# First modulation's shift and scale in column form in one PSUM bank, and the first two feed-forward blocks without their context part and with k outermost

## The chip, the cores and the metric

The kernel runs on one core of one Trainium2 chip. The metric is the device time of one execution in microseconds, taken as the median of several runs. The core has TensorE (PE, with its weight loads PEld), VectorE (DVE), ScalarE (ACT), GpSimd (POOL) and the queue engine SyncE (SP). Each engine works through its own list of instructions in the order in which the program has them, and waits there for what the other engines and the DMA queues owe it.

## The reference, cut to what matters

Two transformer-like blocks follow each other; the change touches only the beginning of the first one.

```python
def modulate(x, shift, scale):
    return x * (1 + scale) + shift

def ada_params(cvec, w, b):
    m = jax.nn.silu(cvec) @ w + b
    return m.reshape(cvec.shape[0], N_ADA, 1, D_MODEL)      # 9 vectors of 1024

def half_ffn(h, shift, scale, gate, g_pre, g_post, w13, w2):
    u = modulate(rmsnorm(h, g_pre), shift, scale)
    return h + 0.5 * gate * rmsnorm(swiglu(u, w13, w2), g_post)
...
        ml = ada_params(c, w_ada[l], b_ada[l])              # for the 512 latent rows x
        mc = ada_params(c_ctx[None], w_ada[l], b_ada[l])    # for the 256 context rows ctx
        h_lat = half_ffn(h_lat, ml[:, 0], ml[:, 1], ml[:, 2], g[0], g[1], w13_a[l], w2_a[l])
        h_ctx = half_ffn(h_ctx, mc[:, 0], mc[:, 1], mc[:, 2], g[0], g[1], w13_a[l], w2_a[l])
```

So before the first big product can run, two slices of `w_ada` (shift, columns 0 to 1023, and scale, columns 1024 to 2047; 1024 rows each, 8 MB together) have to be read and multiplied with two vectors: the SiLU of `c` and of `c_ctx`.

## The kernel before, in words

A matrix product in float32 accuracy is made of three products of float32r halves: each operand is split into a high part (an ACT copy, `wh`, `uh`, `gh`) and a low part (source minus high, usually on DVE, `wl`, `ul`, `gl`). A scheduler writes out the order of each engine's list when the program is built; the order is then fixed.

`setup` makes the columns `sc` (SiLU of `c` and `c_ctx`, 128 x 16). `ffn_a` then runs the startup. Its parts are:

- `ada_start` (lines 192 to 237). It loops over the eight k blocks `kc` of `w_ada`; each brings two tiles of 128 x 1024 from memory, `r1` (scale) and `r0` (shift). The shift is a TensorE product in row form, `adaR`: the two columns of `sc` are the stationary operand and 512 columns of `r0` stream past. The scale is gathered on DVE in `acc1l` and `acc1c`, one multiply-add of 128 x 1024 for each vector and `kc`. After the last `kc`, the rows are copied out (`rows`), turned into columns by eight small transposes (`adaRT`), and the two `acc1` are summed over the partitions: `acc1l` by transposes and a DVE reduction, `acc1c` by eight products with a column of ones (`adaT`). DVE adds the biases and makes the columns `G1l`, `col0l`, `G1c`, `col0c`.
- Interleaved with it, `norm_T` for the four tiles of `x`: a Square with row sum on ACT (`junk`), the inverse root on DVE and POOL (`ntm`, `ntr`), the scaling on DVE (`xn`), eight TensorE transposes (`ntT`), and the copies into `xT`, one half on DVE and one on ACT.
- `ahead` loads and splits the first two weight tiles, their low parts on POOL. The two tiles of `ctx` are normalised on DVE, ACT and POOL right after.
- `modulated` makes `uh` and `ul` from `xT` for one k block after the other: one ACT pass and two DVE passes of 128 x 512.
- `ffn` computes `w13` in blocks `j` of 128 columns, two halves `q` each: `pa` holds 512 latent columns, `pc` 256 context columns. The loops run over `j`, `q`, `kc` and the three partial products. Block 0 first makes its `pa`, then `first()` (transposes and modulation of the context), then its `pc`. From block 1 on, `pa` and `pc` alternate. A `filler` generator puts the work for the other slices of `w_ada` (`acc2l`, `raw_ada`) between the blocks.

From early in block 2 of the feed-forward part on, both kernels have the same instructions in the same order on every engine, to the end of the program.

Of the kernel before, what the change touches and what calls it, by code (L numbers as in the profile page):

```python
# [27 lines left out]
class Net:  # L28
# [32 lines left out]
                self.wpair[i] = self.wsplit(i)  # L61
        return self.wpair.pop(k)

    def ahead(self, n):
        for i in range(n if self.plan else 0):
            tname, off, ap, shp, nm = self.plan[i]
            self.wload(i, bass.AP(tensor=self.tensors[tname], offset=off, ap=ap), shp, nm)
            self.wpair[i] = self.wsplit(i, self.nc.gpsimd)

    def wload(self, k, src, shape, name):  # L70
        raw = self.wr.tile(list(shape), F32, name="raw_" + name, tag="raw")
# [112 lines left out]
        self.nc.sync.dma_start(t, self.scratch[f"row{idx}{w}"])  # L184
        return t

    ONES = "c"
    CE = 0
    MODP = ""
    AH = 2  # L190

    def ada_start(self, pool):
        nc, a = self.nc, self.a
        pb = [self.bank("adaR") for _ in range(2)]
        sc2 = self.sc.rearrange("p (w k) -> p k w", w=2)
        acc = [pool.tile([P, D], F32, name="acc1" + w) for w in "lc"]
        for kc in range(KC):
            r0, r1 = (pool.tile([P, D], F32, name=f"raw_ada{i}", tag="raw", bufs=8) for i in range(2))
            for i, r in ((1, r1), (0, r0)):
                nc.sync.dma_start(r, a["w_ada"][0, kc * P:(kc + 1) * P, i * D:(i + 1) * D])  # L200
            for i in range(2):
                s = self.sc[:, i * 8 + kc:i * 8 + kc + 1]
                if kc == 0:
                    nc.vector.tensor_scalar_mul(acc[i], r1, s)
                else:
                    nc.vector.scalar_tensor_tensor(acc[i], r1, s, acc[i], op0=ALU.mult, op1=ALU.add)
# [10 lines left out]
        ptv = pt[:, 0:16].rearrange("p (k w) -> p w k", w=2)  # L217
        for i, w in enumerate("lc"):
            o, G = (self.const.tile([P, KC], F32, name=n + w) for n in ("col0", "G1"))
            nc.vector.tensor_add(o, ptv[:, i, :], self.bada[:, 0:KC])  # L220
            if w in self.ONES:
                pt = self.bank("adaT")
                for j in range(KC):
                    nc.tensor.matmul(pt[:, j:j + 1], acc[i][:, j * P:(j + 1) * P], self.ones[:, 0:1], start=True, stop=True)
                nc.vector.tensor_add(G, pt[:, 0:KC], self.bada[:, KC:2 * KC])
            else:
                for half in range(2):
                    pt = self.bank("adaT")
                    for j in range(4):
                        kc = half * 4 + j  # L230
                        nc.tensor.transpose(pt[:, j * P:(j + 1) * P], acc[i][:, kc * P:(kc + 1) * P], self.ident)
                    nc.vector.tensor_reduce(G[:, half * 4:half * 4 + 4], pt.rearrange("p (j n) -> p j n", j=4),
                                            axis=AX.X, op=ALU.add)
                nc.vector.tensor_add(G, G, self.bada[:, KC:2 * KC])
# [15 lines left out]
    def norm_T(self, t, x, pool, xT, xn, eng=None):  # L250
        nc = self.nc
        junk = pool.tile([P, D], BF16, name="junk", tag="s")
# [62 lines left out]
    def ffn(self, uh, ul, NT, w13, w2, finish, es, filler=None, rate=0.0, pending=None, lag=1, first=None):  # L315
# [8 lines left out]
        for gi, ng in enumerate(groups):  # L324
# [1 line left out]
            gh, gl = [], []  # L326
            jj = 0
            while jj < ng:
                m = 2 if pending else 1
                cuts = (0, TL // 2, TL) if pending else (0, TL)  # L330
                W, pa, pc = {}, {}, None
                for j in range(j0 + jj, j0 + jj + m):
                    W[j] = [self.weight(w13[:, q * FF + j * P:q * FF + (j + 1) * P].rearrange("(k p) f -> p k f", p=P),
                                        [P, KC, P], "w13") for q in range(2)]
                    pa[j] = [self.bank("pa") for _ in range(2)]
                if ctx:
                    pc = self.bank("pc").rearrange("p (q n) -> p q n", q=2)

                def product(dsts, j, q, kc):
                    h, l = W[j][q]  # L340
# [3 lines left out]
                                             stop=kc == KC - 1 and wi == 2)  # L344

                each = lambda: ((j, q, kc) for j in W for q in range(2) for kc in range(KC))
                for c0, c1 in zip(cuts, cuts[1:]):
                    if c0 > 0:
                        for f in pending:
                            f()  # L350
                        pending = None
                    for j, q, kc in each():
                        product([(pa[j][q][:, c0:c1], slice(c0, c1))] +
                                ([(pc[:, q, :], slice(TL, T))] if ctx and not first else []), j, q, kc)
                if first:
                    first()
                    first = None
                    for j, q, kc in each():
                        product([(pc[:, q, :], slice(TL, T))], j, q, kc)
                for j in W:  # L360
                    s = ev.tile([P, T], F32, name="s", tag="s")
                    g = ev.tile([P, T], F32, name="g", tag="g")
                    h = gp.tile([P, T], F32R, name="gh", tag="gh")
                    l = gp.tile([P, T], F32R, name="gl", tag="gl")
                    nc.scalar.activation(s[:, :TL], pa[j][0], AF.Silu)
                    nc.vector.tensor_mul(g[:, :TL], s[:, :TL], pa[j][1])  # L366
                    if ctx:
                        nc.scalar.activation(s[:, TL:], pc[:, 0], AF.Silu)  # L368
                        nc.vector.tensor_mul(g[:, TL:], s[:, TL:], pc[:, 1])
                    self.split(h, l, g)  # L370
                    gh.append(h)
                    gl.append(l)
# [65 lines left out]
    def ffn_a(self):  # L438
        nc, a, sc = self.nc, self.a, self.scratch
        with ExitStack() as es:  # L440
            self.aux = self.pool(es, "aux", 3)
            xT = self.big_tile([P, KC, TL + TCX], F32, "xT0")
            with ExitStack() as e2:
# [4 lines left out]
                for t in range(4):  # L448
# [4 lines left out]
                    self.norm_T(t, x, sp, xT, sp.tile([P, D], F32, name="xn", tag="xn", bufs=1))()  # L453
                for _ in ada:
                    pass
                self.ahead(self.AH)
                tail = []
                for t in (4, 5):
                    x = sp.tile([P, D], F32, name="xl", tag="xl", bufs=3)
                    nc.sync.dma_start(x, a["ctx"][0, (t - 4) * P:(t - 3) * P, :])  # L460
                    tail.append(self.norm_T(t, x, sp, xT, self.aux.tile([P, D], F32, name="xn", tag="raw"), self.CE and nc.gpsimd))
# [1990 lines left out]
```

## Time and profile before

| | us |
|---|---|
| median of 3 runs (2620.55 to 2624.85) | 2621.93 |
| span of the profiled execution | 2629.1 |
| first product of the feed-forward part starts | 41.07 |
| PE busy over the span | 2464.9 (94%) |

The profile comes from one execution, whose span, from the first to the last instruction, is 2629.1 us; the page gives no other time of that execution. It is 7.2 us above the median of the runs without a profile. Times in the trace count from the start of the span. "PEclk" is the TensorE clock that was granted, as a share of 2.4 GHz: 1.00 is 2.4 GHz, 0.50 is 1.2 GHz.

### The profile page before, as it was taken

Reading aid. Unit: us, or ns where it says so; the run is one execution under the profiler, and the core shown is the slowest. Engines: PE = TensorE matmul, PEld = TensorE weight load, DVE = VectorE, ACT = ScalarE, POOL = GpSimd, SP = SyncE. Lnnn points to the kernel's source line nnn. Section 1 sums busy time; section 2 is a strip of 40 time slices with the busy share of each in tenths; the row PEclk is TensorE's granted clock in tenths of the full one; section 3 lists DMA queues with packets and bytes.
Section 4 is the critical chain, followed back from the end, with each engine's and each line's share of the span. In section 5 each row is a group of like instructions: output and inputs, shape, how many; then the busy total and the mean of one; then the engine's idle time right before and its main releaser. Section 6 shows DMA issues by size and latency. Waiting matters only on the chain. (4 is left out here: it accounts for less than half of the span.)

```text
span 2629.1 us, 32629 instructions
## 1 busy us (share of the span) xinstructions
PE 2464.9 (94%) x12485; PEld 2036.2 (77%) x12485; DVE 1532.1 (58%) x2408; ACT 988.7 (38%) x1785; POOL 495.4 (19%) x487
## 2 busy tenths in 40 slices
PE   7999999998999999999999999998777899996988
PEld 5888888886889889887888887777666687785666
DVE  7554534357557557665433335535696856547899
ACT  4212111125434444434322223435554344322775
POOL 1000000005000000002200002016555434303342
PEclk8999999998999999999999999999888898996999
DMA  7544625344322222154733334448768688664995
GB/s 260 166 152 130 219 64 189 112 153 136 96 75 62 84 73 73 60 171 165 261 92 96 96 96 134 108 93 108 133 121 181 154 149 176 214 220 159 325 332 218
DMA packets 349769, 388.17 MB, mean 148 GB/s; under 512 B 21367, under 2 KB 280924, under 8 KB 349604
## 3 DMA queue, kind: packets, MB, share of 16 engines
q1 hardware_dynamic: 332880, 326.36, 45.5%
q0 software_dynamic: 16544, 59.57, 6.2%
q8 instruction: 100, 1.64, 0.3%
q14 instruction: 65, 0.53, 0.1%
q10 hardware_dynamic: 180, 0.07, 0.0%
HBM read 325.34 MB, written 60.61 MB: 147 GB/s over the span
## 5 line engine op out<-in xcount | busy, mean ns | idle before, releaser
L43 ACT CAST wh<-raw_w 128x1024 fp32r<-128x1024 f32 x132 | 138.2, 1049 | 620.3 <-PE pc L343 233.1
L44 DVE TENSOR_TENSOR wl<-raw_w,wh 128x1024 fp32r<-128x1024 f32 x130 | 159.4, 1229 | 269.8 <-ACT wh L43 267.0
L93 PE MATMUL acc<-wh,gh 128*128 128x512 f32 x440 | 173.9, 395 | 0.0
L94 PE MATMUL acc<-wl,gh 128*128 128x512 f32 x440 | 173.0, 393 | 0.0
L95 PE MATMUL acc<-wh,gl 128*128 128x512 f32 x440 | 172.8, 393 | 0.0
L343 PE MATMUL pa<-u2h,wh 128*128 128x512 f32 (+1 forms) x384 | 145.0, 381 | 5.7 <-ACT u2h L1048 5.7
L343 PE MATMUL pa<-u2h,wl 128*128 128x512 f32 (+1 forms) x384 | 145.8, 380 | 0.0
L343 PE MATMUL pa<-u2l,wh 128*128 128x512 f32 (+1 forms) x384 | 143.9, 375 | 0.0
L343 PE MATMUL pa<-uh,wh 128*128 128x512 f32 x352 | 142.2, 404 | 1.4 <-ACT uh L310 1.4
L343 PE MATMUL pa<-ul,wh 128*128 128x512 f32 x352 | 139.2, 396 | 0.1
L343 PE MATMUL pa<-uh,wl 128*128 128x512 f32 x352 | 138.8, 395 | 0.0
L366 DVE TENSOR_TENSOR g<-s,pa 128x512 f32<-128x512 f32 x44 | 30.2, 686 | 140.6 <-PE pa L343 139.9
L343 PE MATMUL pc<-uh,wh 128*128 128x256 f32 x352 | 98.5, 280 | 0.1
L343 PE MATMUL pc<-ul,wh 128*128 128x256 f32 x352 | 98.4, 280 | 0.0
L1288 DVE SCALAR_TENSOR_TENSOR cv<-padb,cols,cv 128x512 f32<-128x512 f32 x72 | 80.3, 1115 | 31.0 <-ACT cv L1284 30.3
L343 PE MATMUL pc<-uh,wl 128*128 128x256 f32 x352 | 98.3, 280 | 0.0
L93 PEld LDWEIGHTS acc<-wh,gh 128*128 128x128 f32 x440 | 83.2, 189 | 18.3 <-ACT s L368 0.2
L95 PEld LDWEIGHTS acc<-wh,gl 128*128 128x128 f32 x440 | 82.8, 189 | 18.7 <-DVE gl L44 0.5
L94 PEld LDWEIGHTS acc<-wl,gh 128*128 128x128 f32 x440 | 83.1, 189 | 18.3 <-issue 0.2
L2132 DVE TENSOR_TENSOR mwl<-mgu,mwh 128x1024 fp32r<-128x1024 f32 x50 | 80.9, 1627 | 14.6 <-ACT mwh L2131 14.4
L343 PEld LDWEIGHTS pa<-u2h,wh 128*128 128x128 f32 x384 | 73.0, 192 | 19.2 <-ACT u2h L1048 6.2
L343 PEld LDWEIGHTS pa<-u2l,wh 128*128 128x128 f32 x384 | 73.4, 191 | 15.4 <-DVE u2l L1049 0.5
(944 smaller groups left out, 7273.2 us busy)
## 6 DMA issues: line engine op xcount, KB each, us to landing
raw_ada<-in_w_ada SPq DMA_DIRECT2D x72, 512.0 KB, 5.0
raw_w<-in_w_a SPq DMA_DIRECT2D x66, 512.0 KB, 3.9
raw_w<-in_w_b SPq DMA_DIRECT2D x66, 512.0 KB, 3.8
mdn<-in_expert_w_down SPq DMA_DIRECT2D x16, 1024.0 KB, 6.8
mgu<-in_expert_w_gate SPq DMA_DIRECT2D x16, 1024.0 KB, 8.2
mgu<-in_expert_w_up SPq DMA_DIRECT2D x16, 1024.0 KB, 11.9
raw_wg<-in_w_in SPq DMA_DIRECT2D x16, 512.0 KB, 3.8
raw_wo<-in_w_out SPq DMA_DIRECT2D x16, 512.0 KB, 6.7
```

The source lines that it names most:

```text
L43: self.nc.scalar.copy(hi, src)
L44: (eng or self.nc.vector).tensor_sub(lo, src, hi)
L93: self.nc.tensor.matmul(out, ah, bh, start=start, stop=False)
L94: self.nc.tensor.matmul(out, ah, bl, start=False, stop=False)
L95: self.nc.tensor.matmul(out, al, bh, start=False, stop=stop)
L343: nc.tensor.matmul(dst, w[:, kc, :], u[:, kc, c], start=kc == 0 and wi == 0, stop=kc == KC - 1 and wi == 2)
L366: nc.vector.tensor_mul(g[:, :TL], s[:, :TL], pa[j][1])
L1288: nc.vector.scalar_tensor_tensor(t, pad[:, i:i + TL], w[i], t, op0=ALU.mult, op1=ALU.add)
L2132: (nc.gpsimd if i == 2 and e < 13 and n >= 4 or n in self.PRE else nc.vector).tensor_sub(l, x, h)
```

## The change

`ada_start` keeps one PSUM bank, `adaC`, for the whole modulation. The shift tile is now the stationary operand: for each `kc`, eight products load 128 x 128 of `r0` and stream the two columns of `sc` past it, so that the result is in column form. For `kc` 0 to 6 the scale is gathered on DVE as before; after `kc` 6 both `acc1` are added into the same bank by sixteen products with a column of ones; for `kc` 7 the scale tile goes through TensorE like the shift tile. Two additions read the bank out (`mod0l`, `mod0c`).

For the four tiles of `x`, the scaling `xn` and both copies into `xT` move from DVE to ACT (argument `dve=False`). The first weight tile is asked for ahead of the last pair of `w_ada` tiles, the second behind it, and their low parts are made on DVE. The two tiles of `ctx` are loaded early and normalised in `first()`, in place. The first pass of `ffn` now takes blocks 0 and 1 together: their `pa` with `kc` outside `q`, then `first()`, then their `pc`.

```diff
     def ahead(self, i0, i1):
...
-            self.wpair[i] = self.wsplit(i, self.nc.gpsimd)
+            self.wpair[i] = self.wsplit(i)
...
+    DVE_KC = 7
...
+        def by_pe(r, i, kc):
+            for b in range(KC):
+                nc.tensor.matmul(cols(i, b), r[:, b * P:(b + 1) * P], sc2[:, kc, :], start=i == kc == b == 0, stop=False,
+                                 skip_group_check=True)
+
         for kc in range(KC):
...
-            for hf in range(2):
-                nc.tensor.matmul(pb[hf][0:2, :], sc2[:, kc, :], r0[:, hf * 512:hf * 512 + 512],
-                                 start=kc == 0, stop=kc == KC - 1)
+            rs = [pool.tile([P, D], F32, name=f"raw_ada{i}", tag="raw", bufs=8) for i in range(2)]
+            for i in ((1, 0) if kc < self.DVE_KC else (0, 1)):
+                nc.sync.dma_start(rs[i], a["w_ada"][0, kc * P:(kc + 1) * P, i * D:(i + 1) * D])
+            by_pe(rs[0], 0, kc)
+            if kc >= self.DVE_KC:
+                by_pe(rs[1], 1, kc)
+            else:
+                for i in range(2):
...
+                    if kc == self.DVE_KC - 1:
+                        for b in range(KC):
+                            nc.tensor.matmul(cols(1, b)[:, i:i + 1], acc[i][:, b * P:(b + 1) * P], self.ones[:, 0:1],
+                                             start=False, stop=False, skip_group_check=True)
             yield
-        rows = pool.tile([2, D], F32, name="rows")
-        nc.vector.tensor_copy(rows[:, 0:512], pb[0][0:2, :])
-        nc.scalar.copy(rows[:, 512:], pb[1][0:2, :])
-        pt = self.bank("adaRT")
-        for kc in range(KC):
-            nc.tensor.transpose(pt[:, kc * 2:kc * 2 + 2], rows[:, kc * P:(kc + 1) * P], self.ident[:2, :2])
...
+            og = self.const.tile([P, 2, KC], F32, name="mod0" + w)
+            nc.vector.tensor_tensor(og, pv[:, i], self.bada[:, 0:2 * KC].rearrange("p (i k) -> p i k", i=2), op=ALU.add)
+            o, G = og[:, 0, :], og[:, 1, :]
             nc.vector.scalar_tensor_tensor(G, G, 1.0, self.ng[:, 0:KC], op0=ALU.add, op1=ALU.mult)
...
-        (eng or nc.vector).tensor_scalar_mul(xn, x, r)
+        if dve:
+            nc.vector.tensor_scalar_mul(xn, x, r)
+        else:
+            nc.scalar.mul(xn, x, r)
...
-                if half == 0:
+                if half == 0 and dve:
                     nc.vector.tensor_copy(dst, src)
                 else:
                     nc.scalar.copy(dst, src)
...
-                m = 2 if pending else 1
+                m = 2 if pending or first else 1
...
+                first_order = lambda: ((j, q, kc) for j in W for kc in range(KC) for q in range(2))
...
-                    for j, q, kc in each():
+                    for j, q, kc in each() if not first else first_order():
...
+                for j in W:
+                    s = ev.tile([P, T], F32, name="s", tag="s")
+                    g = ev.tile([P, T], F32, name="g", tag="g")
+                    out[j] = s, g
+                    act(j, s, g, slice(0, TL), pa[j])
                 if first:
                     first()
                     first = None
...
+                for _ in range(4):
+                    next(ada)
+                self.ahead(0, 1)
+                next(ada)
+                self.ahead(1, 2)
+                xc = [self.aux.tile([P, D], F32, name="xc", tag="raw") for _ in range(2)]
...
             def first():
-                for f in tail:
-                    f()
+                junk = self.aux.tile([P, D], F32, name="junkc", tag="raw")
+                for t in range(2):
+                    self.norm_T(t + 4, xc[t], None, xT, xc[t], junk=junk)()
                 self.modulated(xT, uh, ul, *self.LC[1])
```

The list of PE in the startup, before: row-form products (`adaR`), transposes of `x` (`ntT`), and the turn into columns at its end, up to the first products of the feed-forward part (`pa`).

```order
L208 MATMUL adaR<-raw_ada_194,sc 2x512
L263 MATMUL ntT<-ident,xn 128x128 x8
L208 MATMUL adaR<-raw_ada_225,sc 2x512 x2
L208 MATMUL adaR<-raw_ada_233,sc 2x512 x2
L208 MATMUL adaR<-raw_ada_241,sc 2x512 x2
L208 MATMUL adaR<-raw_ada_249,sc 2x512 x2
L208 MATMUL adaR<-raw_ada_257,sc 2x512 x2
L216 MATMUL adaRT<-ident,rows 128x2 x4
L231 MATMUL adaT<-ident,acc1l 128x128 x8
L224 MATMUL adaT<-ones,acc1c 128x1 x8
L216 MATMUL adaRT<-ident,rows 128x2 x4
L343 MATMUL pa<-uh,wh 128x512 x2
```

The same list now, from the products of `kc` 1 on (`raw_ada_168` is `kc` 1's shift tile, `_320` and `_321` are `kc` 7's shift and scale tiles).

```order
L200 MATMUL adaC<-sc,raw_ada_168 128x2 x8
L259 MATMUL ntT<-ident,xn 128x128 x16
L200 MATMUL adaC<-sc,raw_ada_205 128x2 x8
L259 MATMUL ntT<-ident,xn 128x128 x8
L200 MATMUL adaC<-sc,raw_ada_242 128x2 x8
L200 MATMUL adaC<-sc,raw_ada_256 128x2 x8
L200 MATMUL adaC<-sc,raw_ada_270 128x2 x8
L200 MATMUL adaC<-sc,raw_ada_284 128x2 x8
L219 MATMUL adaC<-ones,acc1l 128x1 x8
L219 MATMUL adaC<-ones,acc1c 128x1 x8
L200 MATMUL adaC<-sc,raw_ada_320 128x2 x8
L200 MATMUL adaC<-sc,raw_ada_321 128x2 x8
```

Where two products of 512 columns stood for each `kc`, there are eight of 2 columns, each with a stationary tile of its own, and the sixteen products with `ones` stand ahead of the last two groups instead of behind them.

The list of ACT in the startup, before: Squares (`junk`), copies of transposed tiles (`xT`), the first weight casts and the first modulation (`uh`).

```order
L254 ACTIVATE junk,ss<-xl 128x1024
L269 COPY xT_98<-ntT 128x4x128
L254 ACTIVATE junk,ss<-xl 128x1024
L269 COPY xT_98<-ntT 128x4x128
L254 ACTIVATE junk,ss<-xl 128x1024
L269 COPY xT_98<-ntT 128x4x128 x2
L43 CAST wh<-raw_w_308 128x1024
```

The same stretch now, with the scaling of `x` (`xn`) on this engine; the SiLU that makes `sc` stands two rows ahead of the first of these.

```order
L247 ACTIVATE junk,ss<-xl 128x1024
L265 COPY xT_98<-ntT 128x4x128
L252 ACTIVATE xn<-xl,ntr 128x1024
L265 COPY xT_98<-ntT 128x4x128 x3
L247 ACTIVATE junk,ss<-xl 128x1024
L252 ACTIVATE xn<-xl,ntr 128x1024
L265 COPY xT_98<-ntT 128x4x128 x2
L247 ACTIVATE junk,ss<-xl 128x1024
L252 ACTIVATE xn<-xl,ntr 128x1024
L265 COPY xT_98<-ntT 128x4x128 x2
L43 CAST wh<-raw_w_314 128x1024
```

The Square of the third tile of `x` now stands behind the copies of the second tile's transposes, and the Square of the fourth behind those of the third.

The list of DVE where the context part begins, now: the end of block 0's `pa` (`g`), the normalisation of `ctx` (`ntm`, `xc`), filler work (`acc2l`, `acc2c`), the copies of the context's transposes (`xT`) and its modulation.

```order
L356 TENSOR_TENSOR g<-s,pa 128x512
L104 TENSOR_SCALAR ntm<-ss 128x1 x2
L250 TENSOR_SCALAR xc<-xc,ntr 128x1024 x2
L158 TENSOR_SCALAR acc2l<-raw_ada_701,sc 128x1024
L158 TENSOR_SCALAR acc2c<-raw_ada_701,sc 128x1024
L160 SCALAR_TENSOR_TENSOR acc2l<-raw_ada_705,sc,acc2l 128x1024
L160 SCALAR_TENSOR_TENSOR acc2c<-raw_ada_705,sc,acc2c 128x1024
L356 TENSOR_TENSOR g<-s,pa 128x512
L263 COPY xT_98<-ntT 128x4x128 x2
L160 SCALAR_TENSOR_TENSOR acc2l<-raw_ada_709,sc,acc2l 128x1024
L308 TENSOR_SCALAR xT_98<-xT_98,mod0c_353 128x256 x2
L309 TENSOR_TENSOR ul<-xT_98,uh 128x256 x2
```

Before, the first filler work (`acc2l`) stood behind the whole modulation of the context; now five of its passes stand ahead of it.

## Rows read from the trace of the kernel before

**Rows 1.** The page: busy us and share of the span by engine, with the count of instructions.
```profile
PE   2464.9 (94%) x12485; PEld 2036.2 (77%) x12485; DVE 1532.1 (58%) x2408; ACT 988.7 (38%) x1785; POOL 495.4 (19%) x487
```

**Rows 2.** Timeline, first 25 us: start, duration, engine, line, tiles, count, idle before.
```profile
5.56 0.18 ACT L254 ACTIVATION_READ_ACCUMULATOR junk<-xl 128x1 f32 x1
...
5.78 0.15 DVE L104 TENSOR_SCALAR ntm<-ss 128x1 f32<-128x1 f32 x1 [5.78 <-ACT junk L254]
6.08 0.56 POOL L105 TENSOR_TENSOR ntr<-ntm,mhalf 128x1 f32<-128x1 f32 x1 [4.58 <-DVE ntm L104]
...
7.49 1.69 PEld L263 LDWEIGHTS ntT<-ident,xn 128*128 128x128 f32 x8
...
9.51 3.50 PE L208 MATMUL adaR<-raw_ada,sc 128*2 128x512 f32 x4
...
14.71 1.52 POOL L105 TENSOR_TENSOR ntr<-ntm,mhalf 128x1 f32<-128x1 f32 x1 [2.72 <-DVE ntm L104]
...
17.08 1.09 PE L263 MATMUL ntT<-ident,xn 128*128 128x128 f32 x8 [0.38 <-DVE xn L256]
...
21.37 7.20 PE L208 MATMUL adaR<-raw_ada,sc 128*2 128x512 f32 x16
```

**Rows 3.** Timeline, 29 to 41 us: from the last tile of w_ada to the first product.
```profile
29.29 0.09 PEld L208 LDWEIGHTS adaR<-raw_ada,sc 128*2 128x2 f32 x2 [1.66 <-DMA raw_ada<-in_w_ada]
...
31.57 1.28 DVE L206 SCALAR_TENSOR_TENSOR acc1c<-raw_ada,sc,acc1c 128x1024 f32<-128x1024 f32 x1
...
35.76 3.41 PE L224 MATMUL adaT<-ones,acc1c 128*128 128x1 f32 x16
...
39.10 0.59 PE L216 MATMUL adaRT<-ident,rows 2*128 2x2 f32 x4
...
41.07 1.22 PE L343 MATMUL pa<-uh,wh 128*128 128x512 f32 x2 [1.38 <-ACT uh L310]
```

**Rows 4.** Windows: PE, PEld, DVE, ACT, POOL busy, granted clock, DMA share, GB/s.
```profile
34.00:46.00 12.00, 10.54 (x42) 9.03 (x42) 5.33 (x15) 5.80 (x10) 4.46 (x4) 0.50 0.63 190
752.00:753.00 1.00, 1.00 (x10) 1.00 (x10) 0.16 (x1) 0.52 (x3) 0.33 (x1) 1.00 0.21 55
754.00:756.00 2.00, 2.00 (x11) 2.00 (x11) 0.00 (x0) 1.14 (x4) 0.00 (x0) 0.50 0.90 265
2324.00:2326.00 2.00, 1.96 (x16) 1.86 (x16) 0.61 (x1) 0.77 (x3) 0.00 (x0) 1.00 0.79 220
```

**Rows 5.** Timeline, 752 to 761 us, PE alone.
```profile
752.40 0.27 PE L93 MATMUL S<-qh,kh 128*128 128x128 f32 x1
752.51 0.28 PE L94 MATMUL S<-ql,kh 128*128 128x128 f32 x1
...
756.10 0.41 PE L94 MATMUL S<-ql,kh 128*128 128x128 f32 x1
756.31 0.41 PE L95 MATMUL S<-qh,kl 128*128 128x128 f32 x1
756.53 0.73 PE L561 MATMUL wg<-u1h,wh 128*128 128x512 f32 x1
...
760.41 0.40 PE L561 MATMUL wg<-u1h,wh 128*128 128x512 f32 x1
```

**Rows 6.** Timeline, 2324 us: products of 20 columns.
```profile
2324.02 1.96 PE L1816 MATMUL rbias<-wrt,gbc 128*128 128x20 f32 x16 [0.70 <-DVE gbc L1813]
```

**Rows 7.** Groups of instructions, startup: count, then busy us and mean ns of one.
```profile
L254 ACT ACTIVATE junk<-xl 128x1024 bf16<-128x1024 f32 x4 | 4.2, 1058 | 5.6 <-DMA xl<-in_x 5.6
L269 ACT COPY xT<-ntT 128x512 f32<-128x512 f32 x4 | 2.3, 580 | 3.5 <-PE ntT L263 3.5
```

**Rows 8.** Timeline of ACT: SiLU on the context part of blocks 1, 2 and 3.
```profile
80.95 0.37 ACT L368 ACTIVATE s<-pc 128x256 f32<-128x256 f32 x1
97.75 0.38 ACT L368 ACTIVATE s<-pc 128x256 f32<-128x256 f32 x1
114.55 0.38 ACT L368 ACTIVATE s<-pc 128x256 f32<-128x256 f32 x1
```

More of the change, by code (lines that the diff above doesn't have):

```diff
@@ L62, in weight, with ahead @@
         return self.wpair.pop(k)
-    def ahead(self, n):
-        for i in range(n if self.plan else 0):
+    def ahead(self, i0, i1):
+        for i in range(i0, i1 if self.plan else i0):
             tname, off, ap, shp, nm = self.plan[i]
             self.wload(i, bass.AP(tensor=self.tensors[tname], offset=off, ap=ap), shp, nm)
-            self.wpair[i] = self.wsplit(i, self.nc.gpsimd)
+            self.wpair[i] = self.wsplit(i)
     def wload(self, k, src, shape, name):
@@ L185, in row @@
         return t
-    ONES = "c"
-    CE = 0
     MODP = ""
     AH = 2
+    DVE_KC = 7
     def ada_start(self, pool):
         nc, a = self.nc, self.a
-        pb = [self.bank("adaR") for _ in range(2)]
+        pb = self.bank("adaC")
+        cols = lambda i, b: pb[:, (i * KC + b) * 2:(i * KC + b) * 2 + 2]
         sc2 = self.sc.rearrange("p (w k) -> p k w", w=2)
         acc = [pool.tile([P, D], F32, name="acc1" + w) for w in "lc"]
+        def by_pe(r, i, kc):
+            for b in range(KC):
+                nc.tensor.matmul(cols(i, b), r[:, b * P:(b + 1) * P], sc2[:, kc, :], start=i == kc == b == 0, stop=False,
+                                 skip_group_check=True)
@@ L197, in ada_start @@
         for kc in range(KC):
[L198 to L206, printed above, removed]
@@ L217, in ada_start @@
-        ptv = pt[:, 0:16].rearrange("p (k w) -> p w k", w=2)
-        for i, w in enumerate("lc"):
[L219 to L234, printed above, removed]
+            rs = [pool.tile([P, D], F32, name=f"raw_ada{i}", tag="raw", bufs=8) for i in range(2)]
@@ L248, in slab8, with norm_T @@
         return self.mr.tile(shape, dtype, name=name, tag="dn", bufs=3)
-    def norm_T(self, t, x, pool, xT, xn, eng=None):
+    def norm_T(self, t, x, pool, xT, xn, dve=True, junk=None):
         nc = self.nc
-        junk = pool.tile([P, D], BF16, name="junk", tag="s")
+        if junk is None:
+            junk = pool.tile([P, D], BF16, name="junk", tag="s")
         ss = self.sm.tile([P, 1], F32, name="ss", tag="ss")
@@ L328, in ffn @@
             while jj < ng:
-                m = 2 if pending else 1
+                m = 2 if pending or first else 1
                 cuts = (0, TL // 2, TL) if pending else (0, TL)
-                W, pa, pc = {}, {}, None
+                W, pa, pc = {}, {}, {}
                 for j in range(j0 + jj, j0 + jj + m):
                     W[j] = [self.weight(w13[:, q * FF + j * P:q * FF + (j + 1) * P].rearrange("(k p) f -> p k f", p=P),
-                                        [P, KC, P], "w13") for q in range(2)]
+                                        [P, KC, P], "w13", 1 if first else None) for q in range(2)]
                     pa[j] = [self.bank("pa") for _ in range(2)]
-                if ctx:
-                    pc = self.bank("pc").rearrange("p (q n) -> p q n", q=2)
+                    if ctx:
+                        pc[j] = self.bank("pc").rearrange("p (q n) -> p q n", q=2)
                 def product(dsts, j, q, kc):
@@ L351, in ffn, with act @@
                         pending = None
-                    for j, q, kc in each():
+                    for j, q, kc in each() if not first else first_order():
                         product([(pa[j][q][:, c0:c1], slice(c0, c1))] +
-                                ([(pc[:, q, :], slice(TL, T))] if ctx and not first else []), j, q, kc)
+                                ([(pc[j][:, q, :], slice(TL, T))] if ctx and not first else []), j, q, kc)
+                out = {}
+                def act(j, s, g, c, x):
+                    nc.scalar.activation(s[:, c], x[0], AF.Silu)
+                    nc.vector.tensor_mul(g[:, c], s[:, c], x[1])
+                for j in W:
[3 more added lines that the diff above has]
+                    act(j, s, g, slice(0, TL), pa[j])
                 if first:
@@ L452, in ffn_a @@
                     nc.sync.dma_start(x, a["x"][0, t * P:(t + 1) * P, :])
-                    self.norm_T(t, x, sp, xT, sp.tile([P, D], F32, name="xn", tag="xn", bufs=1))()
+                    self.norm_T(t, x, sp, xT, sp.tile([P, D], F32, name="xn", tag="xn", bufs=2), False)()
+                for _ in range(4):
[5 more added lines that the diff above has]
+                for t in range(2):
+                    nc.sync.dma_start(xc[t], a["ctx"][0, t * P:(t + 1) * P, :])
                 for _ in ada:
                     pass
[L456 to L461, printed above, removed]
                 uh, ul = (self.big_tile([P, KC, TL + TCX], F32R, n) for n in ("uh", "ul"))
@@ L465, in first @@
             def first():
-                for f in tail:
-                    f()
+                junk = self.aux.tile([P, D], F32, name="junkc", tag="raw")
+                for t in range(2):
+                    self.norm_T(t + 4, xc[t], None, xT, xc[t], junk=junk)()
                 self.modulated(xT, uh, ul, *self.LC[1])
```

16 lines of the change are left out of this document (9 added, 7 removed).

## The prediction

> **What bounds the kernel now.** I read the page first. PE is busy for 94% of the span [rows 1], and the change touches only the startup and the first two blocks of the feed-forward part; behind them both programs have the same lists. So the question is one number: how much later or earlier PE reaches block 2. A shift there goes through to the end, since nothing in this program waits for a fixed time.
>
> Then I read the timeline of the startup. Before, its end is a chain. The last tile of `w_ada` is there at 29.29, DVE's last multiply-add ends at 31.57 + 1.28 = 32.85, and then come the copies, transposes and sums, up to the last `adaRT` transposes at 39.10 + 0.59 = 39.69; the first product of the feed-forward part starts at 41.07, 1.38 later [rows 3]. Between the last tile and the last transposes lie 10.4 us, and of these the reader may expect the column form to save most: with the result already in columns, little is left to do behind the last load.
>
> The last thing that I read is the clock, and it decides the case. The first four `adaR` rows take 3.50 us, 0.88 each, and sixteen later ones 7.20, or 0.45 each [rows 2]: by their durations the first run at 1.2 GHz and the later ones at 2.4. From 34 to 46 us, where PE does transposes, the products with `ones` and the first products of block 0, and is busy for most of the time, the granted clock is 0.50 throughout [rows 4].
>
> **The price of a column-form product.** The nearest rows are the eight products with `ones` for `acc1c`: a 128 x 128 float32 tile as stationary operand and one column past it. They are 16 rows (two for each float32 product) and take 3.41 us, 0.213 for a row, at the granted clock of 0.50 [rows 3, 4]. At 1.00 the sixteen `rbias` rows with 20 columns take 1.96, 0.1225 for a row [rows 4, 6]. The weight load sets this pace, not the columns. So eight such products cost 3.41 us at half clock and 1.96 at the full one.
>
> The new startup has 9 groups of eight with `raw_ada` (eight for the shift, one for `kc` 7's scale) and 2 with `ones`: 88 products, 176 rows. At half clock they cost 11 x 3.41 = 37.5 us, at the full one 21.6. The 32 transposes come on top: 1.69 of loads for eight at half clock, 1.09 for eight at the full one [rows 2].
>
> **Which clock they get.** Before, the products that went ahead of the first full-clock rows were the 512-column `adaR`, and these are gone; what is left is transposes and products of one or two columns. The trace has a plain case of this at 752 us. Products of 128 columns follow each other without any gap, PE busy 1.00 and loads 1.00 of each microsecond, and in the middle of it the clock falls from 1.00 to 0.50: a product every 0.11 us at 752.4 and every 0.21 at 756.1 [rows 4, 5]. It is back only after some 3.9 us of 512-column products (756.53 to 760.41) [rows 5]. Together with 34 to 40 us, where products of this very kind ran at 0.50 to the end, it makes me take half clock for the whole startup.
>
> The Trainium skill speaks against this. TensorE: Matmul & The Clock Gate, Part 1 (The HAM clock gate), says that sustained activity releases the throttle and that the instructions are not counted, so an uninterrupted stream of small products would warm the clock as well as any. By that rule PE, busy without a break, would be at 2.4 GHz for most of the startup; the result is the first rival below. The trace does not agree: the unbroken stretch at 752 us lost the full clock. The same page, LDWEIGHTS (loading the stationary operand), gives a load of 128 columns as 128/1.2 = 107 ns; by it the 176 rows would cost an estimated 18.8 us. The rows at half clock have twice that, and the rows decide.
>
> **The startup step by step, at half clock.** The first transposes wait for `xn` from ACT: `ntr` ends at 6.08 + 0.56, an ACT pass of 128 x 1024 takes 1.06 [rows 2, 7], so PE starts at 7.85, has eight transposes until 9.55, `kc` 0 until 12.96, `kc` 1 until 16.37, and the transposes of the second tile until 18.07, the last of them ending some 0.2 later. Now the order bites. The third tile's transposes are next on PE, and ACT's Square of that tile stands behind the copies of the second tile's transposes. PE waits for: a copy 0.58, the Square 1.06 and its sum 0.19, `ntm` 0.15, `ntr` 0.56 to 1.52, the scaling 1.06 [rows 2, 7], and about 0.5, an estimate, for five hand-overs: 4.1 to 5.1, taken as 4.6. It resumes at 22.9 and has the transposes until 24.6 (ending 24.8) and `kc` 2 until 28.0; the fourth tile's chain of 4.6 ends at 29.4. Transposes until 31.1, four groups for `kc` 3 to 6 until 44.7, the two groups with `ones` until 51.6, `kc` 7 twice until 58.4.
>
> The loads don't hold this up: the last tile was there at 29.29 before [rows 3]; now it comes later, since its buffer is released by `kc` 3's products at about 34.5, and a `w_ada` tile landing even 6 us after that is there long before 51.6. What is taken off DVE (four `xn`, four copies, two multiply-adds, the two reductions) is worth nothing here, since PE ends last; the same holds for the low parts that move from POOL to DVE, made under PE's 30 us of products.
>
> From the last product to the first of the feed-forward part I keep the 1.38 of before: 59.8 in place of 41.07, **+18.7 us**. Bounds: without either wait of PE for ACT, 6.2 less (+12.5); with the longer chain twice, about 1 more; at the full clock's price of a row, the first rival below.
>
> **Blocks 0 and 1.** A block takes 114.55 - 97.75 = 16.8 at full clock [rows 8], and the context's sixteen transposes 2.2: 35.8 for two blocks. Before, from 41.07 to the SiLU at 80.95 [rows 3, 8] are 39.9, so 4.1 are lost; most of that is the half clock, which lasts to 46 us at least [rows 4], and waits for `uh` and `ul`. Now the same price of the clock comes again: 3.9 us of dense products in one case [rows 5], at least 4.9 in the other (41.07 to 46), so about 4.4 at half speed, 2.2 lost. With `kc` outside `q` each k block feeds six products, so PE waits less for the modulation; I put the first products' waits at 1.0 (0 to 2, an estimate). Before the context's products PE waits for the copies, ACT and DVE, and DVE's list has a filler pass there whose load goes through one buffer three times in a row: 2.5 (1 to 4, an estimate). With 0.4 until the SiLU the loss is 6.1, against 4.1: **+2.0**. So the k-outermost order gives back what it can, and the new wait for the context takes it again.
>
> **The sum.** 18.7 + 2.0 = +20.7 us. The profiled span is 2629.1, 7.2 above the median; with the change it should read about 2650. On the median that is 2621.9 + 20.7 = **2642.6**, its own range 2635 to 2649.
>
> **The rivals.**
>
> *The full clock in the startup.* `kc` 0 at half clock until 12.96, from there 1.96 for a group and 1.0 for eight transposes: `kc` 1 until 14.9, transposes until 15.9, ACT's chain until 20.6, transposes 21.6, `kc` 2 23.6, chain until 26.3, transposes 27.3, four groups 35.1, two with `ones` 39.1, two for `kc` 7 43.0. That is +3.3 against 39.69, and -0.2 in the blocks, which start warm: 2625. For it: that PE would have no idle stretch from 27 us on. Against it: the two stretches above [rows 4, 5]. It is not slower by what can be told: 0.2%, or 5.2 us, is about what a measurement of this kernel tells from no change. It decides where a group of eight costs about 2.0 in place of 3.4. It is also what the rule of the Trainium skill above would give in this kernel.
>
> *The full clock, and ACT's chain hidden too.* The two waits (4.7 and 2.7) go: the last product at 35.6, -4.1, and -0.2 in the blocks: 2617.6. Even so it is faster by less than 0.2%; for more, PE's rows would have to be cheaper than any row of the trace. I see no such row.
>
> *The clock rises on the way*, say at 31 us, when the long unbroken run begins: the last 27.3 us shrink by 0.1225/0.213 to 15.7, and the blocks start warm: 20.7 - 11.6 - 2.2 = +6.9, 2629. Against it: from 34 to 40 us, 6 us of the same kind did not raise it [rows 4].
>
> *The wait for the context grows*: 3 us more if the filler's load lands late, 2646; inside the range.
>
> **How the numbers follow.** Main case 0.80; full clock 0.09; clock rising on the way 0.07; faster by over 0.2% by something that I don't see 0.04. Slower by over 0.2% is the first and the third, 0.87; the same 0.09; faster 0.04. The range is 2629 to 2649: it holds the main case with its bounds and the lower edge of the third case, and leaves out the other two.
>
> **What would show it.** Right: in the changed profile the `adaC` rows come every 0.21 us to the end, at a granted clock of 0.50 where the trace records one; PE has gaps of 4 to 5 us near 18 us and of 1 to 2 near 28; the last `adaC` row ends at 57 to 60 and the first `pa` row starts about 1.4 later; the SiLU on the context of block 2 starts near 118 instead of 97.75, and everything behind it has the same distance. Wrong: `adaC` rows every 0.12 us, a last one near 43, or a first `pa` row before 45.

## The result, and the profile after

The changed kernel takes 2641.51 us, the median of 10 runs (2634.97 to 2650.04), against 2623.40 for 10 runs of the kernel before beside it (2610.41 to 2633.52). The ratio is 1.0077, its 95% interval 1.0059 to 1.0095, that is 15.5 to 24.9 us slower, 20.2 by the ratio itself; the two medians differ by 18.1. The prediction was 2642.6 with a range of 2629 to 2649.

The page's line of busy time, as in [rows 1] for before:

```profile
PE 2474.1 (94%) x12597; PEld 2060.7 (78%) x12597; DVE 1526.9 (58%) x2395; ACT 994.3 (38%) x1792; POOL 491.9 (19%) x485
```

PE is busy for 9.2 us more, PEld for 24.5: the new products are weight loads above all.

The timeline of PE from the first transposes to the first product of the feed-forward part (start, duration, engine, line, operation, tiles, count, idle before); it answers to [rows 2, 3]:

```profile
7.76 1.97 PE L259 MATMUL ntT<-ident,xn 128*128 128x128 f32 x8
9.52 6.83 PE L200 MATMUL adaC<-sc,raw_ada 128*128 128x2 f32 x32
16.20 1.95 PE L259 MATMUL ntT<-ident,xn 128*128 128x128 f32 x8
22.86 1.97 PE L259 MATMUL ntT<-ident,xn 128*128 128x128 f32 x8 [4.71 <-ACT xn L252]
24.62 3.41 PE L200 MATMUL adaC<-sc,raw_ada 128*128 128x2 f32 x16
29.53 1.97 PE L259 MATMUL ntT<-ident,xn 128*128 128x128 f32 x8 [1.50 <-ACT xn L252]
31.30 13.65 PE L200 MATMUL adaC<-sc,raw_ada 128*128 128x2 f32 x64
44.81 3.55 PE L219 MATMUL adaC<-ones,acc1l 128*128 128x1 f32 x16
48.22 3.55 PE L219 MATMUL adaC<-ones,acc1c 128*128 128x1 f32 x16
51.64 6.96 PE L200 MATMUL adaC<-sc,raw_ada 128*128 128x2 f32 x32
59.98 0.79 PE L339 MATMUL pa<-uh,wh 128*128 128x512 f32 x1 [1.38 <-ACT uh L306]
```

A group of 16 rows costs 3.41 us wherever it stands, also in the stretch from 31.30 to 58.60, in which PE has no gap at all. PE is the engine that ends last: in DVE's timeline the first sum behind the products waits for them, for 21.24 us.

```profile
58.64 0.17 DVE L225 TENSOR_TENSOR mod0l<-adaC,cols 128x16 f32<-128x16 f32 x1 [21.24 <-PE adaC L200]
```

Then PE in block 0, where the full clock comes back (a product every 0.43 us up to 65, every 0.23 from there), and the turn to the context, with a wait of 1.17 behind the sixteen transposes:

```profile
64.44 0.63 PE L339 MATMUL pa<-ul,wh 128*128 128x512 f32 x1
64.86 0.53 PE L339 MATMUL pa<-uh,wl 128*128 128x512 f32 x1
65.24 0.39 PE L339 MATMUL pa<-ul,wh 128*128 128x512 f32 x1
65.47 0.39 PE L339 MATMUL pa<-uh,wl 128*128 128x512 f32 x1
...
85.30 1.91 PE L259 MATMUL ntT<-ident,xc 128*128 128x128 f32 x16
88.38 0.50 PE L339 MATMUL pc<-uh,wh 128*128 128x256 f32 x2 [1.17 <-ACT uh L306]
```

ACT's timeline, the SiLU on the context of blocks 0, 1 and 2 (before: [rows 8], block 2 at 97.75):

```profile
99.31 0.37 ACT L355 ACTIVATE s<-pc 128x256 f32<-128x256 f32 x1
...
103.47 0.37 ACT L355 ACTIVATE s<-pc 128x256 f32<-128x256 f32 x1
...
118.00 0.38 ACT L355 ACTIVATE s<-pc 128x256 f32<-128x256 f32 x1
```

So the first product is 18.9 us later and block 2 20.25 us. The profiled spans differ by less, 2638.3 against 2629.1: 11 us of the shift are not there at the end of this execution. The last experiments are about them.

### The profile page after: what moved, and what is told of

Its sections match the earlier page's. It is cut to its first block, busy times and chain, and to the rows that moved or that the text cites. A ratio compares the mean times of both kernels' runs of the same rounds, so it can differ in the third digit from the quotient of the medians.

```text
span 2638.3 us, 32844 instructions
## 1 busy us (share of the span) xinstructions
PE 2474.1 (94%) x12597; PEld 2060.7 (78%) x12597; DVE 1526.9 (58%) x2395; ACT 994.3 (38%) x1792; POOL 491.9 (19%) x485
## 5 line engine op out<-in xcount | busy, mean ns | idle before, releaser
L93 PE MATMUL acc<-wh,gh 128*128 128x512 f32 x440 | 173.6, 395 | 0.0
L95 PEld LDWEIGHTS acc<-wh,gl 128*128 128x128 f32 x440 | 82.6, 188 | 18.8 <-DVE gl L44 0.5
L2139 DVE TENSOR_TENSOR mwl<-mgu,mwh 128x1024 fp32r<-128x1024 f32 x50 | 80.9, 1627 | 14.7 <-ACT mwh L2138 14.5
L339 PEld LDWEIGHTS pa<-u2h,wh 128*128 128x128 f32 x384 | 72.4, 190 | 19.2 <-ACT u2h L1055 6.1
```

The lines of the kernel that those rows point to most:

```text
L93: self.nc.tensor.matmul(out, ah, bh, start=start, stop=False)
L95: self.nc.tensor.matmul(out, al, bh, start=False, stop=stop)
L339: nc.tensor.matmul(dst, w[:, kc, :], u[:, kc, c], start=kc == 0 and wi == 0, stop=kc == KC - 1 and wi == 2)
L2139: (nc.gpsimd if i == 2 and e < 13 and n >= 4 or n in self.PRE else nc.vector).tensor_sub(l, x, h)
```

## Experiments

The table holds what each run's profile and its times show. "Rest" is the span less the time of block 2's SiLU, and "at 0.50" the part of the rest in which the granted clock is 0.50, added up over the clock events of the trace. Times against before are the ratio and its 95% interval, turned into us by the median of the runs of before beside it. before2, again and warm2 are further profiles of the kernel before, the changed kernel and warm.

| kernel | first product | SiLU, block 2 | rest | at 0.50 | time against before, us |
|---|---|---|---|---|---|
| before | 41.07 | 97.75 | 2531.4 | 196.3 | |
| before2 | 39.20 | 95.11 | 2527.3 | 183.7 | |
| rowform | 39.42 | 99.47 | 2529.2 | 186.6 | +4.7 (1.6 to 7.6) |
| changed | 59.98 | 118.00 | 2520.3 | 177.0 | +20.2 (15.5 to 24.9) |
| again (the changed kernel) | 60.01 | 117.40 | 2504.0 | 150.4 | +19.2 (12.3 to 26.0) |
| colonly | 56.04 | 118.31 | 2521.2 | 186.1 | +17.6 (14.2 to 21.0) |
| prewarm | 57.97 | 116.61 | 2515.3 | 172.7 | +14.2 (10.5 to 18.1) |
| warm | 60.46 | 120.33 | 2496.5 | 136.1 | +7.1 (1.8 to 12.3) |
| warm2 (the same) | 60.41 | 119.86 | 2510.6 | 173.6 | |
| dve8 | 56.44 | 114.94 | 2512.5 | 168.0 | +10.5 (6.3 to 14.4) |
| normdve | 54.23 | 111.42 | 2524.2 | 184.4 | +6.6 (2.9 to 10.0) |
| both | 50.96 | 109.97 | 2522.6 | 184.4 | +3.4 (0.0 to 6.8) |
| qouter | 59.85 | 117.27 | 2517.4 | 174.3 | +16.5 (11.5 to 21.3) |
| delay | 59.81 | 116.57 | 2524.5 | 197.6 | +12.6 (7.9 to 17.3) |

**Which part of the change: rowform and colonly.**

```diff
 # rowform: the changed kernel
-    ada_start with by_pe (column form)
+    ada_start of the kernel before (adaR, adaRT, adaT)
-    xn ... bufs=2
+    xn ... bufs=1     (room for the tile rows)
 # colonly: the kernel before
-    ada_start with adaR, adaRT, adaT
+    ada_start with by_pe, DVE_KC = 7
```

> The startup's modulation is computed in row form again, as before the change; the norms' scaling on ACT, the k-outermost order and the two blocks without ctx stay. My theory (PE's 88 column-form products at 0.21 us a row make the loss): the first product of the feed-forward part starts at 40 to 42 us in place of 59.98, the SiLU on the context of block 2 at 97 to 101, and the time is -2 to +3 us against the kernel before. Rival, the norm's chain on ACT makes the loss: the first product stays behind 47, time +6 or more. Rival, the new order of the first two blocks makes it: the first product at 41, but block 2 more than 5 us late.

> The kernel before with the column form alone. My theory: adaC rows 0.21 us apart, first product of the feed-forward part at 57 to 62 us, time +16 to +21 against the kernel before. Rival, the move of the norms to ACT makes part of the loss: first product before 55, time under +13.

PE in rowform; all of the last 20 adaR rows are one run, and the eight products with `ones` (16 rows) that took 3.41 us in [rows 3] take 1.95:

```profile
24.72 8.75 PE L208 MATMUL adaR<-raw_ada,sc 128*2 128x512 f32 x20
...
36.29 1.95 PE L224 MATMUL adaT<-ones,acc1c 128*128 128x1 f32 x16
39.42 1.22 PE L347 MATMUL pa<-uh,wh 128*128 128x512 f32 x2 [1.18 <-ACT uh L314]
```

Without the column form the 18.9 us are gone, so neither the norms on ACT nor the new loads make them. Block 2 came where my theory had it and the first product 0.6 us before its range; the time is above what it allowed (+4.7 in place of at most +3). Against the second profile of before, block 2 is 4.4 us late, which is nearer to that time. In colonly the products end at 53.1, earlier than in the changed kernel, since PE hardly waits for the norms there; then PE waits 2.95 us for a weight's high part, and the two blocks take longer (62.3 us from the first product to block 2's SiLU; 58.0 in the changed kernel):

```profile
27.44 1.97 PE L257 MATMUL ntT<-ident,xn 128*128 128x128 f32 x8 [1.11 <-DVE xn L250]
...
46.12 6.97 PE L202 MATMUL adaC<-sc,raw_ada 128*128 128x2 f32 x32
56.04 0.79 PE L337 MATMUL pa<-uh,wh 128*128 128x512 f32 x1 [2.95 <-ACT wh L43]
```

The first product lies 1 us below my expectation; block 2 (+20.6) and the time are the changed kernel's within the intervals. The column form alone makes nearly all of the loss; the rest of the change costs 1.7 us at block 2 of rowform by the first profile of before, 4.4 by the second.

**Whether it is the clock: prewarm and warm.** Both add products of 512 bf16 columns whose results nobody uses.

```diff
 # prewarm: the changed kernel
+        self.warm(10)
         nc.tensor.transpose(pt[:, 0:16], cc, ...)
+        self.warm(4)
         nc.tensor.transpose(pt[:, 16:136], v1, ...)
+        self.warm(4)
 # warm: the changed kernel, in by_pe, and the same in the loop with ones
                 nc.tensor.matmul(cols(i, b), r[:, b * P:(b + 1) * P], sc2[:, kc, :], ...)
+                if b % 2:
+                    self.warm(1)
```

> The changed kernel with 18 products of 512 bf16 columns (results unused) ahead of the first transposes, where PE is idle, so that the startup's own products begin at the full clock. My theory: the column-form products do not keep it; the first groups have rows 0.12 us apart, the later ones 0.21; first product of the feed-forward part at 55 to 60, time 0 to -5 against the changed kernel (+13 to +18 against before). Rival, the clock stays once it is up: all rows at 0.12, first product at 43 to 48, time within 5 us of before.

> The changed kernel with one product of 512 bf16 columns (result unused) behind every second column-form product, 44 in all. My theory, the clock sets the row price: from the second or third group on the rows are 0.12 us apart (a group of eight with its four extra products 2.8 us in place of 3.41), first product of the feed-forward part at 50 to 54, and with blocks that begin at the full clock the time is +7 to +12 against before. Rival, the weight load has this price whatever the clock: rows stay at 0.21, first product at 60 or later, time +18 or more.

In prewarm the startup begins at the full clock: eight transposes take 1.04 us in place of 1.97. Within the first column-form group it is lost, and it doesn't come back before the feed-forward part. The timeline of PE:

```profile
8.45 1.04 PE L270 MATMUL ntT<-ident,xn 128*128 128x128 f32 x8
11.26 3.08 PE L211 MATMUL adaC<-sc,raw_ada 128*128 128x2 f32 x16 [1.77 <-ACT sc L147]
...
15.94 3.41 PE L211 MATMUL adaC<-sc,raw_ada 128*128 128x2 f32 x16
```

And two windows of prewarm (PE, PEld, DVE, ACT, POOL busy, granted clock, DMA share, GB/s):

```profile
12.00:52.00 40.00, 37.00 (x175) 36.83 (x175) 16.66 (x17) 10.15 (x16) 3.08 (x2) 0.50 0.71 245
30.00:56.00 26.00, 26.00 (x123) 26.00 (x124) 5.40 (x5) 1.17 (x2) 0.00 (x0) 0.50 0.53 164
```

In 40 us with the loads busy for 36.83 the granted clock is 0.50 throughout, also in the second window, in which PE has no gap. First product (57.97) and time (+14.2) lie where my theory had them; the clock did not even last for the first groups, as it allowed. The Trainium skill, TensorE: Matmul & The Clock Gate, Part 1 (The HAM clock gate), lets sustained activity release the throttle and does not count the instructions; for these products the trace doesn't agree.

In warm my theory expected more than came: the first product is at 60.46, not at 50 to 54. The scheduler did not leave the extra products where I put them; up to 33 us they stand singly and the rows stay slow, then ten and thirteen stand together. PE's timeline:

```profile
32.80 4.28 PE L194 MATMUL dm<-wm 128*128 128x512 bf16 x10
36.91 1.84 PE L208 MATMUL adaC<-sc,raw_ada 128*128 128x2 f32 x16
38.62 2.97 PE L194 MATMUL dm<-wm 128*128 128x512 bf16 x13
...
46.12 2.73 PE L229 MATMUL adaC<-ones,acc1l 128*128 128x1 f32 x16
48.70 3.55 PE L229 MATMUL adaC<-ones,acc1c 128*128 128x1 f32 x16
```

Windows of warm, one in each state:

```profile
36.00:46.00 10.00, 10.00 (x69) 7.47 (x68) 0.00 (x0) 0.00 (x0) 0.00 (x0) 1.00 0.45 154
48.00:58.00 10.00, 10.00 (x48) 10.00 (x48) 0.00 (x0) 0.00 (x0) 0.00 (x0) 0.50 0.17 42
```

Between the extra products the same 16 rows cost 1.84 us. The clock column reads 1.00 there, but the trace has no clock event before the fall near 47 us; it is the rows' durations that show the full clock. At 46.12 the extra products stop, the clock falls within the next sixteen rows, and a group costs 3.55. So the price is the clock's, which the rival (a load of this price at any clock) denied. At 7.1 the time lay at the lower edge of the range that I gave, but not for my reason: the startup gained nothing, the rest of this execution is the shortest of all (2496.5). As a repair the extra products came too late and stopped too early.

**The rows and the waits by themselves: dve8, normdve, both.**

```diff
 # dve8
-    DVE_KC = 7
+    DVE_KC = 8
 # normdve
-    self.norm_T(t, x, sp, xT, sp.tile(..., bufs=2), False)()
+    self.norm_T(t, x, sp, xT, sp.tile(..., bufs=2))()
 # both: the two together
```

> The changed kernel with the scale of the last k block on DVE as well: eight column-form products, 16 rows, fewer. My theory (PE ends last, 0.213 us a row): the last adaC row ends 3.4 us earlier, near 55.2, the first product of the feed-forward part at 56.6, time -3 to -4 against the changed kernel (+14 to +17 against before). Rival, DVE's chain or the loads end last: the first product stays at 59 to 60.

> The changed kernel with the scaling of xn and the first copy of each tile on DVE again, as before the change. My theory: PE's two waits for ACT (4.7 and 1.5 us) all but go, since DVE has room; last adaC row near 53, first product at 54 to 55, time -4 to -6 against the changed kernel (+11 to +15 against before). Rival, the norms end as late on DVE, behind its multiply-adds: the first product stays at 58 to 60.

> The changed kernel with both edits: the last scale block on DVE, and the norms' scaling on DVE. My theory: the two add up, first product at 50.5 to 52, time -8 to -10 against the changed kernel (+8 to +12 against before): the column form still loses, since 160 rows at 0.213 are 34 us. Rival, DVE becomes the bound: first product at 54 or later.

PE in normdve; of the two waits for `xn` one of 1.11 is left, and the last products begin 5.7 us earlier:

```profile
27.26 1.97 PE L259 MATMUL ntT<-ident,xn 128*128 128x128 f32 x8 [1.11 <-DVE xn L250]
...
45.95 6.97 PE L200 MATMUL adaC<-sc,raw_ada 128*128 128x2 f32 x32
```

The first product is 3.5 us earlier in dve8 (16 rows at 0.213 are 3.4), 5.75 in normdve, and 9.0 in both, where the two add up within 0.3: PE ends last, and each row and wait taken from it counts. The times gained more than that: by the table 10, 14 and 17 us against the changed kernel, where 3 to 4, 4 to 6 and 8 to 10 were expected. With some 6 us either way on such a difference dve8 is compatible, normdve and both are not; what their times gained beyond the startup isn't shown. Even so none of them is faster than the kernel before, nor is rowform; no version of the runs beats it.

**The k-outermost order: qouter.**

```diff
-first_order = lambda: ((j, q, kc) for j in W for kc in range(KC) for q in range(2))
+first_order = lambda: ((j, q, kc) for j in W for q in range(2) for kc in range(KC))
```

> The changed kernel with q outside k in the first two blocks, so that a k block of uh and ul feeds three products in place of six. My theory: PE starts at 60 as in the changed kernel and waits some 1 to 2 us more for uh and ul; block 2's SiLU on the context 0 to 2 us later than 118.0; time within 3 us of the changed kernel. Rival, the k-outermost order is worth more than the prediction gave it: 4 us or more later.

From the first product to block 2's SiLU are 57.4 us; in the two profiles of the changed kernel 58.0 and 57.4. Block 2 is 0.7 us earlier than in the first of these, where my theory had 0 to 2 later and the rival 4 or more. The order of q and k makes no difference that can be seen: PE waits 0.52 us for `ul` in either.

**Whether a shift goes through: delay, again, before2, warm2.**

```diff
 # delay: the kernel before
-                for j in range(KC):
+                for j in list(range(KC)) * 7:
                     nc.tensor.matmul(pt[:, j:j + 1], acc[i][:, j * P:(j + 1) * P], self.ones[:, 0:1], ...)
```

> The kernel before with one thing added: the eight products with ones for acc1c are issued seven times over (the same result each time), 96 more rows at some 0.213 us, so that all behind the startup comes about 20 us later and nothing else is changed. If a shift of the startup goes through to the end, as the prediction says: block 2's SiLU on the context near 118, time +19 to +22. Rival, part of any such shift is given back later, where TensorE's clock falls at other places: the same SiLU near 118, time +10 to +16, and fewer us at the granted clock of 0.50 behind block 2 than in the kernel before.

> The changed kernel once more, beside the delayed one. By the prediction's step: +18 to +21 against before. If the falls of the clock behind block 2 go by where the work stands, its profile has them at the same places as the first one (877, 979 and 1085 us, none near 773); if they are chance, at others.

> The kernel before once more, for a second profile. If the falls of the clock go by where the work stands, they come at 753, 859, 965 and 1070 us again; if they are chance, at others, and the span differs from 2629.1 by about half of the difference in time at half clock.

> The kernel with 44 extra products of 512 columns once more, for a second profile. If its startup is the same in each execution: first product of the feed-forward part at 60 to 61 again. If the moment at which the clock rises differs between executions, as its times (2613 to 2643) let one think: a startup that differs by several us.

The delay is 18.8 us at block 2, and the time grows by 12.6, at most 17.3: the expectation of +19 to +22 is not met, the rival's size is. Its mechanism is not: behind block 2 the clock is at 0.50 for 197.6 us, against 196.3 and 183.7 in the two profiles of before. ACT's rows are 18.1 to 20.1 us later than before's up to 1825 us of before, 14.3 at 1854 and 12.0 at 2600. Between 1825 and 1854 us POOL's product `Mm` waits for a load from a scratch tensor. POOL's timeline in before:

```profile
1854.85 1.29 POOL L1458 TENSOR_TENSOR Mm<-Mpl,m 128x512 f32<-128x512 f32 x1 [11.35 <-DMA Mpl<-scr_Mp]
```

And in delay:

```profile
1869.15 1.28 POOL L1458 TENSOR_TENSOR Mm<-Mpl,m 128x512 f32<-128x512 f32 x1 [6.47 <-DMA Mpl<-scr_Mp]
```

The load is issued at 1840.19 and at 1858.17, so it took 14.7 us in the one and 11.0 in the other. In the three profiles whose block 2 comes before 100 us this wait of POOL is 9.3 to 11.4, 10.2 on the mean; in the eleven others 4.6 to 8.9, 6.9 on the mean. The start of block 2 is not all that tells the two groups apart: by the pages the three have 12485 instructions on PE and the eleven 12581 to 12641. No run is late without the longer list, so which of the two shortens the wait is not shown.

The table lets the clock's share be taken out. As an estimate, work at 0.50 loses half of its time; the rest less half of the column "at 0.50" is 2433 to 2436 us in the three early profiles and 2424 to 2432 in the eleven late ones. On the mean the rest of the late ones is 13.9 us shorter, of which this puts 7.9 to the clock and 6.0 to something else; the wait for `Mpl` is 3.3 of that.

The profile of again is the other half. Its startup and first blocks are those of the changed kernel within 0.6 us, yet its span is 2621.4, 16.9 us less. Windows over three stretches of products of 128 columns, as those of [rows 5], in the changed kernel (the granted clock is the third column from the end):

```profile
877.00:887.00 10.00, 10.00 (x49) 8.61 (x49) 3.84 (x8) 4.17 (x9) 0.00 (x0) 0.83 0.17 51
979.00:989.00 10.00, 10.00 (x44) 8.91 (x44) 2.64 (x4) 2.65 (x8) 0.08 (x1) 0.66 0.28 80
1085.00:1095.00 10.00, 10.00 (x61) 10.00 (x61) 4.80 (x10) 3.02 (x8) 0.00 (x0) 0.66 0.00 1
```

The same stretches in again:

```profile
874.00:884.00 10.00, 10.00 (x62) 8.77 (x62) 3.50 (x7) 4.22 (x11) 0.55 (x1) 1.00 0.29 80
974.00:984.00 10.00, 10.00 (x58) 7.99 (x57) 3.86 (x5) 5.05 (x12) 0.55 (x1) 1.00 0.44 126
1077.00:1087.00 10.00, 10.00 (x80) 9.22 (x79) 5.40 (x11) 4.69 (x13) 0.00 (x0) 1.00 0.10 29
```

The same products lost the clock three times in one execution and never in the other; at 1090 us the second is 7.4 us ahead. On the mean the granted clock is 0.966 and 0.971, which is some 14 us of the 16.9 (2638.3 x 0.034 less 2621.4 x 0.029). So a fall can come in one execution of a program and be missing in the next. The places are not random, though. Before has falls near 753 [rows 4], 859, 965 and 1071 us; in before2 the first of them is missing, and the other three come at the same work (855, 957, 1063). Of these four places eleven of the 14 profiles have three or four falls, and again, warm and dve8 have none. In the startup of before2, on PE, the eight products with `ones` (16 rows) lose the clock on their way and take 2.55 in place of 3.41, and the first product comes 1.9 us earlier than in the first profile.

```profile
34.76 2.55 PE L224 MATMUL adaT<-ones,acc1c 128*128 128x1 f32 x16
...
39.20 0.79 PE L343 MATMUL pa<-uh,wh 128*128 128x512 f32 x1 [1.38 <-ACT uh L310]
```

warm2 answers its question with no: the startup is the same (60.41), and the spread of its times has to come from behind, where its rest is 14 us longer than in the first profile, with 173.6 us at 0.50 in place of 136.1.

## Why the prediction was right, and where not

- **The price of a row and its clock.** Right: 3.41 us for 16 rows, and the loss goes where the column form goes (rowform, colonly, dve8). The sign "a granted clock of 0.50" could not be read in the changed kernel, whose trace has no clock event in the startup; prewarm's trace has one, and there rows of this price stand at 0.50.
- **The order on PE.** Right within 0.3 us: the waits for ACT ended at 22.86 and 29.53 (22.9 and 29.4), the last product at 58.60 (58.4), the first of the feed-forward part at 59.98 (59.8), 1.38 later.
- **Blocks 0 and 1, +2.0.** Measured +1.34. The half clock lasted 5.0 us (4.4), the first waits were 0.52 (1.0), the wait at the context's turn 1.17 (2.5). That "the k-outermost order gives back what it can" is not borne out: qouter shows that it gives nothing that can be seen.
- **"A shift there goes through to the end, since nothing in this program waits for a fixed time."** This step failed. The span did not read 2650 but 2638.3, and 2621.4 in the second profile; a bare delay of 18.8 us cost 12.6. Two things stand in its place. Behind block 2 a fall of the clock comes in one execution and is missing in the next at the same work, worth some 14 us between two profiles of one program; of the 11 us that are missing in the changed kernel's first profile some 9.6 are the clock's by the estimate above (177.0 us at 0.50 in place of 196.3). And in all eleven late profiles the rest is shorter also without the clock, by 6.0 us on the mean, 3.3 of it at the wait for `Mpl`; in delay, where the clock gives nothing back, this is all that is missing. Why that wait is shorter, and whether lateness or the longer list of PE does it, stays open, and so does whether the clock's part is luck.
- **The time.** It came out within 1.1 us of the forecast, closer than this step deserves. The forecast was added to 2621.93; the runs of before beside the changed kernel have a median of 2623.40, so that the increase is 18.1 by the medians, not 20.7. And the second profile of before has its block 2 2.6 us earlier, which makes the shift 22.9 us; what is given back behind hides that. So the agreement of the number is in part luck.
- **The rivals.** A full clock in the startup, and one that rises on the way, did not come, in an unbroken stretch of 27 us; the context's wait didn't grow. ACT's chain cost 5.75 us, as normdve shows, and would not have turned the sign: both still is not faster than before.

## What to carry to other kernels

Before turning a product so that the long operand becomes the stationary one, ask which clock the new products will run at. At the same clock the two forms cost the same here for a k block: at 0.50, 3.50 us as four rows of 512 moving columns and 3.41 as sixteen rows of two columns; at the full clock 1.80 (a quarter of the 7.20 in [rows 2]) and 1.84 (warm). But the rows of 512 columns ran at the full clock from the second k block on, and the sixteen rows did not keep it even when it was given to them. Eleven groups at 3.41 in place of 1.84 are 17.3 us, an estimate, and that is most of the 18.9. And where the clock falls by chance, compare kernels at a landmark near the change first; one profile's span says little about the rest, which differed by 16.3 us between two profiles of one kernel.

## What was not expected of the hardware

The clock that is granted to the same work differs between executions: 0.966 and 0.971 on the mean for the changed kernel's two profiles. The Trainium skill, TensorE: Matmul & The Clock Gate, Part 1 (The HAM clock gate), says of a kernel's first products that their slow stretch differs from run to run. The two profiles of before agree with it: their first four `adaR` rows take 3.50 and 3.01 us. In the changed kernel, whose products stay at the price of the half clock, the first product of the feed-forward part comes within 0.1 us of the same time, and it is the stretches far behind that differ. The clock column can mislead: in the changed kernel it reads 1.00 for 31 to 58 us, where the rows have the durations of prewarm's at 0.50; the trace has no event there before the first fall, at 635 us, so it is the durations that count.
